# An eight-expert SwiGLU at the end of a two-layer trunk: on-chip memory laid out from a rehearsal, expert weights in rows of 4 and 8 KB, four jobs an expert, a light place first

## The chip, the cores and the metric

One Trainium2 chip, of which the kernel uses one core. A core has five engines that run their own instruction streams side by side: TensorE (PE, matrix products; its weight loads are shown as PEld), VectorE (DVE), ScalarE (ACT), GpSimd (POOL) and SyncE (SP). Here SP issues the loads of weights from HBM into SBUF, the on-chip memory; 16 DMA engines carry them out. Products land in eight PSUM banks. The metric is the device time of one execution in microseconds (us), lower is better.

## The reference, cut to what matters

Two layers of a trunk over 256 context rows and 256 latent rows of width 1024. All of it is in float32.

```
for layer in range(2):                       # layer 1 is the last: latent rows alone from its mixer on
    x = x + g1 * mixer(modulate(rms_norm(x)))
    h = modulate(rms_norm(x))                # 256 x 1024
    layer 0:  x = x + g2 * (silu(h @ w_gate) * (h @ w_up)) @ w_down           # width 2816
    layer 1:  logits = h @ router            # 8 experts, the best two of each row
              gates  = softmax of the two best logits
              for e in range(8):             # w_gate, w_up: 1024 x 3584, w_down: 3584 x 1024
                  out += gates[:, e] * (silu(h @ w_gate[e]) * (h @ w_up[e])) @ w_down[e]
              x = x + g2 * out
return rms_norm(x) * final_norm_g
```

The three matrices of an expert have 44.0 MB, those of the eight experts 352.3 MB. On the inputs that the reference draws, its routing sends 49, 84, 60, 51, 58, 61, 72 and 77 rows to the experts 0 to 7.

## The kernel before

The kernel is written as generators (a mixer, a dense feed-forward, the expert stage `moe`) that a planner, `drive`, interleaves while the program is built. The planner keeps a clock of its own and decides from it the order in which instructions stand on each engine. What waits for what on the chip is settled by semaphores, from the buffers that instructions share.

**Places.** The experts are worked off in eight places, one after the other. A place is heavy (H) or light (L), as `KIND` says, and the places go H L H L H L H L. An H place has room for 128 rows, an L place for 64. The routing (`route`) sorts the experts by how many rows they have; `RANK` tells which place takes which in that order. Expert 0 always comes first in it and has the first place, so that its weights can be loaded before the routing is known (the address of every other place's weights comes from a register that SP loads after the sort, `numbers`). If an expert has more rows than its place has room for, `overflow` computes the rest at the end, behind a branch.

**An H place** multiplies in three products of float32r values: a weight tile `raw` is cut into a high part `wh` (an ACT cast) and a low part `wl` (a DVE subtraction), and the rows likewise (`xeh`, `xel`); `cut_next` and `cut_rest` do this in pieces of 128x1024, of which four are kept (`PIECES`). **An L place** multiplies the float32 weights straight from `raw`, gate and up side by side in the two halves of the array (`pairs`), without cuts.

**Jobs.** A place is seven jobs of 512 of the 3584 hidden columns. A job computes gate and up over eight blocks k of 128 rows (`lin` or `pairs`, into one bank each or one bank in all), then silu on ACT, a product on DVE, and four transposes to the hidden rows' layout (`flip`, bank `pht`), which the second block of the next job's gate carries along (`aside`); `down` multiplies the hidden rows of the job before into the place's banks `y`. Between the blocks `beside` hands in small work: `combine` adds a finished place to the tokens (bank `pcb`), `gather` picks the next place's rows (bank `pxe`).

**Loads.** `moe_units` makes a list of loads of 1 MB, in the order of use: gate and up tiles of 4 blocks by 512 columns (each of the 128 partitions reads four rows of 2 KB), down tiles of 2 blocks by 1024 columns (two rows of 4 KB). `loads` issues the next as soon as there is a buffer. Buffers come from pools: `raws` (4 tiles of 128x2048), one more from `raws2` in layer 1, and, once `early` is set in the second mixer, four tiles of 128x512 from the pool `acts` (63 tiles, which hold activations otherwise) in place of one `raw`; such a load is then issued as four of 128x512, 256 KB each, with rows of 2 KB (`flex`). `SPARE` and `AMAX` bound how many.

```
            if self.free_raw or self.free_raw2:
                self.load(u)
            elif self.early and u["flex"] and self.ACTS - self.live >= 4 + SPARE[self.ap] and self.aheld < AMAX[self.ap]:
                self.aheld += 1
                ...
                u["raw"] = [self.act(name="raw2") for _ in srcs]
```

Every instruction that the planner records on DVE or ACT has line L101, matmuls L244, most transposes L258, loads L202.

## Time and profile before

| | us |
|---|---|
| median of 3 runs | 1777.2 |
| the runs | 1775.42 to 1777.76 |
| the profiled execution's own time | 1777.62 |
| its span, from first to last instruction | 1775.8 |

The profile lists busy time of each engine over the span, and in any stretch of it; what a wait of an engine ended; how much the DMA engines moved; and in order of time what ran. A matmul's end is modelled, so that a short wait inside a run of matmuls can be hidden in busy time. In names such as `gu<-raw,u` the tile written stands left of the arrow. A load's duration on SP is that of its issue.

### The profile page before, as it was taken

What the parts mean: (1) busy time and instruction counts of PE and PEld (TensorE: products, weight loads), DVE (VectorE), ACT (ScalarE), POOL (GpSimd) and SP (SyncE); (2) the same over time, 40 slices, a digit from 0 to 9 for tenths busy, and PEclk for the clock granted to TensorE, in tenths of its full rate; (3) what the DMA queues carried; (4) which work ended last, traced back from release to release, by engine and by line L of the source; (5) the groups of instructions that cost most, each with busy time, mean ns of one, the idle gap of its engine ahead of it and who ended that gap; (6) DMA issues with size and microseconds to landing.
All of it is one profiled execution on the core that took longest, in us unless ns stands there. A gap on an engine that the chain in (4) does not pass through costs nothing. (4 is left out here: it accounts for less than half of the span.)

```text
span 1775.8 us, 25616 instructions
## 1 busy us (share of the span) xinstructions
PE 1713.2 (96%) x8283; PEld 1214.1 (68%) x8283; DVE 1170.0 (66%) x2139; ACT 844.1 (48%) x1620; POOL 2.3 (0%) x9
## 2 busy tenths in 40 slices
PE   7999998999999999999899999999999998999985
PEld 3876776888888888977788536884358842588431
DVE  6899988888764345778699406983069930598412
ACT  3467654444222224566588315872058720477311
POOL 0000000000000000000000000000000000000000
PEclk9899998999999998999999999999999999999999
DMA  9531234456873333226699999999999999999996
GB/s 307 182 129 54 84 125 149 136 170 186 285 242 121 96 89 99 82 95 221 246 357 360 349 392 390 389 379 380 391 389 391 389 387 392 388 373 390 393 387 242
DMA packets 284377, 470.69 MB, mean 265 GB/s; under 512 B 24120, under 2 KB 92236, under 8 KB 284236
## 3 DMA queue, kind: packets, MB, share of 16 engines
q1 hardware_dynamic: 284076, 468.46, 73.8%
q8 instruction: 67, 1.10, 0.3%
q14 instruction: 74, 0.61, 0.1%
q0 software_dynamic: 160, 0.52, 0.1%
HBM read 467.86 MB, written 1.05 MB: 264 GB/s over the span
## 5 line engine op out<-in xcount | busy, mean ns | idle before, releaser
L101 ACT CAST wh<-raw 128x512 fp32r<-128x512 f32 (+4 forms) x708 | 499.9, 743 | 369.7 <-PE pp L244 221.1
L101 DVE TENSOR_TENSOR wl<-raw,wh 128x512 fp32r<-128x512 f32 (+4 forms) x708 | 562.1, 842 | 130.6 <-ACT wh L101 120.3
L244 PE MATMUL gu<-raw,u 128*64 128x512 f32 x896 | 223.3, 604 | 13.2 <-DMA raw<-in_moe_w_up_dram 9.5
L244 PE MATMUL pp<-hh,wh 128*128 128x512 f32 (+1 forms) x592 | 230.2, 389 | 1.5 <-ACT hh L101 1.5
L244 PE MATMUL pp<-hl,wh 128*128 128x512 f32 (+1 forms) x592 | 225.6, 381 | 0.2 <-DVE hl L101 0.2
L244 PE MATMUL pp<-hh,wl 128*128 128x512 f32 (+1 forms) x592 | 225.7, 381 | 0.0
L101 DVE SCALAR_TENSOR_TENSOR macc<-mt,sc,macc 128x512 f32<-128x512 f32 x240 | 169.3, 748 | 27.9 <-DMA mt<-in_w_mod_dram 27.1
L244 PEld LDWEIGHTS gu<-raw,u 128*64 128x64 f32 x896 | 61.7, 137 | 125.3 <-issue 76.8
L101 DVE TENSOR_TENSOR sg<-sg,gu 64x512 f32<-64x512 f32 x28 | 19.4, 692 | 171.4 <-ACT sg L101 171.3
L244 PEld LDWEIGHTS pp<-hh,wh 128*128 128x128 f32 x592 | 112.8, 191 | 23.8 <-ACT hh L101 1.9
L244 PEld LDWEIGHTS pp<-hh,wl 128*128 128x128 f32 x592 | 112.5, 190 | 21.9
L244 PEld LDWEIGHTS pp<-hl,wh 128*128 128x128 f32 x592 | 112.9, 191 | 21.2 <-DVE hl L101 0.7
L244 PE MATMUL y<-raw,hT 128*64 128x512 f32 x448 | 107.3, 596 | 6.4 <-DMA raw<-in_moe_w_down_dram 4.7
L244 PE MATMUL g<-wh,xeh 128*128 128x512 f32 x224 | 92.9, 415 | 1.8 <-ACT wh L101 1.7
L244 PE MATMUL g<-wl,xeh 128*128 128x512 f32 x224 | 87.9, 393 | 3.1 <-DVE wl L101 3.1
L244 PE MATMUL g<-wh,xel 128*128 128x512 f32 x224 | 87.9, 393 | 1.5 <-DVE xel L101 1.5
L244 PE MATMUL u<-wh,xeh 128*128 128x512 f32 x224 | 88.0, 393 | 0.0
L244 PE MATMUL y<-wh,hTh 128*128 128x512 f32 x224 | 87.6, 391 | 0.0
L244 PE MATMUL u<-wl,xeh 128*128 128x512 f32 x224 | 87.3, 390 | 0.0
L244 PE MATMUL y<-wl,hTh 128*128 128x512 f32 x224 | 87.2, 389 | 0.0
L244 PE MATMUL u<-wh,xel 128*128 128x512 f32 x224 | 87.2, 389 | 0.0
L244 PEld LDWEIGHTS y<-raw,hT 128*64 128x64 f32 x448 | 33.1, 137 | 72.7 <-issue 52.9
(327 smaller groups left out, 2541.2 us busy)
## 6 DMA issues: line engine op xcount, KB each, us to landing
raw<-in_moe_w_up_dram SPq DMA_DIRECT2D x300, 256.0 KB, 7.3
raw<-in_moe_w_down_dram SPq DMA_DIRECT2D x292, 256.0 KB, 6.9
raw<-in_moe_w_gate_dram SPq DMA_DIRECT2D x280, 256.0 KB, 6.0
mt<-in_w_mod_dram SPq DMA_DIRECT2D x192, 256.0 KB, 3.3
raw<-in_moe_w_gate_dram SPq DMA_DIRECT2D x42, 1024.0 KB, 8.5
raw<-in_moe_w_down_dram SPq DMA_DIRECT2D x39, 1024.0 KB, 7.3
raw<-in_moe_w_up_dram SPq DMA_DIRECT2D x37, 1024.0 KB, 7.9
raw<-in_ffn_w_down_dram SPq DMA_DIRECT2D x16, 704.0 KB, 4.6
```

The costliest lines, as they stand in the source:

```text
L101: return f(out, *args, **kw)
L244: self.nc.tensor.matmul(out, lhsT, rhs, start=start, stop=stop)
```

## The change

- **SBUF.** The pools `raws`, `raws2`, the pool of cut pieces, `acts` and the pool of modulation weights go. One `Arena` of 104 slots of 128x512 takes their place, in 26 tiles of four slots. The program is built twice: in the rehearsal every request for memory gets a place of its own, and the recording wrappers `Seen` note the first and the last instruction that uses it; `lay_out` then gives each request slots that are free over that stretch, and the second build uses them. A load takes one whole tile of four slots; there is no `flex` any more. To make room, the scratch memory for GpSimd's DMAs is cut to 2 KB, and the final norm's gain comes through eight transposes in place of two GpSimd DMAs.
- **How many loads at a time.** Up to the second mixer four, then five, as before. From the point at which `early` was set (now `wide`) `place_raw` counts slots: loads held, cut pieces, live tiles and a reserve (`SPARE`) have to fit in 104.
- **Jobs.** `WIDE = (2, 2, 2, 1)`: three jobs of 1024 hidden columns and one of 512. A gate or up tile has 2 blocks of 1024 columns (rows of 4 KB; in the last job still 4 blocks of 512, rows of 2 KB). A down tile gives each partition two neighbouring rows of the matrix, 8 KB in one piece, 32 KB away from the next partition's (16 KB in the last job); the hidden columns are transposed in the order that fits. A job fills two banks for gate and two for up in an H place, two in all in an L place.
- **Order.** The places go L H L H H L H L, and `RANK` follows: the experts in the first place, and three with the fewest rows, are light.

```diff
-SPARE, AMAX, ROOM = (10, 3, 3), (13, 12, 9), 62
+SLOT, SLOTS, FOURS, SPARE, ROOM = 512, 104, (5, 3), (16, 26, 26), 62
...
-GATHER_AT = 5
+GATHER_AT = 2
...
-GATES_AT, UDVE = 1, (0, 0, 0, 0)
-KIND, CAP = "HLHLHLHL", dict(H=128, L=64)
-RANK = (0, 4, 1, 5, 2, 6, 3, 7)
+GATES_AT = 0
+KIND, CAP = "LHLHHLHL", dict(H=128, L=64)
+RANK = (0, 1, 5, 2, 3, 6, 4, 7)
+WIDE = (2, 2, 2, 1)
...
+class Arena:
...
+    def take(self, n, dt=F32):
+        i = len(self.uses)
+        self.uses.append([n, self.count, self.count, dt == F32R])
+        if self.rehearsal:
+            s, self.top = self.top, self.top + n
+            t = self.all[:, s * SLOT:(s + n) * SLOT].bitcast(dt)
+        else:
+            s, new = self.layout[i]
+            four = s // 4
+            if new:
+                t = self.tiles[four] = self.pool.tile([128, 4 * SLOT], dt, name=f"four{four}", tag=f"four{four}")
+                self.base[t.tensor.name] = four * 4, 4 * SLOT
+            t = self.tiles[four][:, s % 4 * SLOT:(s % 4 + n) * SLOT]
+        for k in range(n):
+            self.at[s + k] = i
+        return t
...
+def lay_out(uses):
...
+    for i in sorted(range(len(uses)), key=lambda i: (uses[i][1], -uses[i][0])):
+        n, a, b, r = uses[i]
+        best = None
+        for s in range(0, SLOTS, n):
+            last, four = max(end[s:s + n]), s // 4
+            till = max(end[4 * four:4 * four + 4])
+            kind = 4 if four >= SLOTS // 4 - FOURS[0] else 2 if four >= SLOTS // 4 - sum(FOURS) else 1
+            if last >= a or a < wide and (n == 4) != (kind == 4) or till >= a and kinds[four] != r:
+                continue
+            soon = max(0, 50 - (a - last))
...
     def load(self, u):
-        u["pool"] = self.raws if self.free_raw else self.raws2
-        u["raw"] = u["pool"].tile([128, 2048], F32, name="raw", tag="raw")
+        u["raw"] = self.arena.take(4)
+        self.held_raws += 1
+        self.to_cut += len(u["pieces"])
...
+    def place_raw(self, u):
+
+        if not self.wide:
+            return self.held_raws < self.RAWS
+        cut = self.cut - len(self.used)
+        if u["pieces"] or self.cut < self.to_cut:
+            cut = self.PIECES
+        return self.held_raws * 4 + cut * 4 + self.live + 4 <= SLOTS - SPARE[self.ap]
...
-        J = [(e, i) for e in range(NE) for i in range(7)]
+        J = [(e, i) for e in range(NE) for i in range(len(WIDE))]
...
+                u = make((G, U)[w], e, s(0, D), s(f0, f0 + n), "(k p) c -> p k c", s(g, g + kts))
+                h[w] += [(u, k) for k in range(kts)]
...
-            us = [make(Dn, e, i * 512 + g * 256, 0, 2, 1024) for g in range(2)]
-            return [(us[k // 2], k % 2) for k in range(4)]
+            f0, n = sum(WIDE[:i]) * 512, WIDE[i] * 512
+            us = [make(Dn, e, s(f0, f0 + n), s(0, D), "(p k) c -> p k c", s(g, g + 2)) for g in range(0, n // 128, 2)]
+            return [(u, k) for u in us for k in range(2)]
...
-        def pairs(p, gate, up, xs, e, j):
+        def pairs(P, gate, up, xs, e, j):
...
-                self.mm(p[0:64], xs[k], wg(kk), k == 0, k == KT - 1)
-                self.mm(p[64:128], xs[k], wu(kk), k == 0, k == KT - 1)
+                for q, p in enumerate(P):
+                    self.mm(p[0:64], xs[k], wg(kk, q), k == 0, k == KT - 1)
+                    self.mm(p[64:128], xs[k], wu(kk, q), k == 0, k == KT - 1)
...
+            for q in range(WIDE[i]):
+                p = self.ps("pht")
                 for f in range(4):
+                    self.tr(p[:, f * 128:(f + 1) * 128], hid[:, q * 4 + f::n])
```

How instructions move is shown at three places. The first is SP, where the loads of the experts' weights begin, in the second mixer. Before, a row is one load, `raw` the buffer; `128x4x512` is a whole tile, `128x512` a quarter of one:

```order
L202 DMA raw<-in_moe_w_gate_dram 128x4x512 x2
L202 DMA raw<-in_moe_w_up_dram 128x4x512
L202 DMA raw_7575<-in_moe_w_up_dram 128x512
L202 DMA raw_7576<-in_moe_w_up_dram 128x512
L202 DMA raw_7577<-in_moe_w_up_dram 128x512
L202 DMA raw_7578<-in_moe_w_up_dram 128x512
L202 DMA raw_7583<-in_moe_w_gate_dram 128x512
```

The same place of SP now; a tile is called `four` and a number, whatever it holds:

```order
L121 DMA four_6263<-in_moe_w_gate_dram 128x2x1024
L121 DMA four_6626<-in_moe_w_up_dram 128x2x1024
L121 DMA four_6652<-in_moe_w_gate_dram 128x2x1024
L121 DMA four_6666<-in_moe_w_up_dram 128x2x1024
...
L121 DMA four_7040<-in_moe_w_gate_dram 128x2x1024
L121 DMA four_7240<-in_moe_w_up_dram 128x2x1024
L121 DMA four_7242<-in_moe_w_down_dram 128x2048
L121 DMA four_7244<-in_moe_w_down_dram 128x2048
L121 DMA four_7246<-in_moe_w_down_dram 128x2048
L121 DMA four_7248<-in_moe_w_down_dram 128x2048
L121 DMA four_7268<-in_moe_w_gate_dram 128x2x1024
```

The quarters have gone; each load is a tile of 1 MB, gate and up in turn, and twenty of them (sixteen of gate and up, four of down) stand ahead of the first that needs a tile which another load of this stage has held.

The second place is PE at the end of the routing, where the first place's rows are gathered (`pxe`) and its gate begins (`g`). Before:

```order
L244 MATMUL ppos<-mb,oneb 128x8
L244 MATMUL pxe<-OH,tok 128x128 x16
L244 MATMUL g<-wh,xeh 128x512
L244 MATMUL g<-wl,xeh 128x512
L244 MATMUL g<-wh,xel 128x512
```

Now:

```order
L121 MATMUL ppos<-mb,oneb 128x8
L121 MATMUL pxe<-four_7145,four_82 128x64
L121 MATMUL pxe<-four_7145,four_75 128x64
...
L121 MATMUL g<-four_6263,four_7145 64x512
L121 MATMUL g<-four_6626,four_7145 64x512
L121 MATMUL g<-four_6263,four_7145 64x512
L121 MATMUL g<-four_6626,four_7145 64x512
```

There are sixteen gathers of 64 rows in place of sixteen of 128, and the matmuls behind them read the loaded tiles (`four_6263` gate, `four_6626` up) without a cut; each block now takes two products with each.

The third place is PE in an H place, the change from a job's up (`u`) to `down` and the next gate, here in the second place, whose `y` rows still belong to the L place before it; `pht` are the transposes. Now:

```order
L121 MATMUL u<-four_7738,four_7567 128x512 x2
L121 MATMUL y<-four_7586,four_82 64x512 x4
L121 MATMUL y<-four_7588,four_82 64x512 x4
L121 MATMUL g<-four_7546,four_7521 128x512 x2
...
L121 MATMUL g<-four_7757,four_7521 128x512 x2
L121 MATMUL g<-four_7546,four_7521 128x512 x2
L121 MATMUL pht<-idf,four_7618 128x128 x8
```

Products come in twos, one for each bank, and eight transposes stand together where four stood before; an H place has 504 products and 28 transposes either way.

## Rows read from the trace of the kernel before


**Rows 1.** The page: span, busy time of the engines, two groups of loads.

```profile
span 1775.8 us, 25616 instructions
PE 1713.2 (96%) x8283; PEld 1214.1 (68%) x8283; DVE 1170.0 (66%) x2139; ACT 844.1 (48%) x1620; POOL 2.3 (0%) x9
...
raw<-in_moe_w_up_dram SPq DMA_DIRECT2D x300, 256.0 KB, 7.3
raw<-in_moe_w_gate_dram SPq DMA_DIRECT2D x42, 1024.0 KB, 8.5
```

**Rows 2.** The eight places (window and length, PE, PEld, DVE, ACT, POOL, clock, DMA, GB/s).

```profile
873.30:993.80 120.50, 117.75 (x558) 97.11 (x556) 112.99 (x175) 96.75 (x154) 0.00 (x0) 1.00 0.92 332
993.80:1081.10 87.30, 87.30 (x419) 33.85 (x418) 18.14 (x28) 17.29 (x30) 0.00 (x0) 1.00 1.04 386
1081.10:1205.40 124.30, 124.30 (x574) 98.70 (x572) 107.78 (x151) 90.91 (x140) 0.00 (x0) 1.00 1.04 385
1205.40:1298.40 93.00, 89.66 (x420) 34.29 (x419) 20.73 (x35) 15.72 (x30) 0.00 (x0) 1.00 1.04 385
1298.40:1425.80 127.40, 125.30 (x574) 98.52 (x572) 109.30 (x156) 92.83 (x146) 0.00 (x0) 1.00 1.05 391
1425.80:1525.20 99.40, 93.44 (x420) 35.38 (x419) 20.71 (x33) 15.04 (x27) 0.00 (x0) 0.98 1.04 389
1525.20:1653.10 127.90, 125.11 (x572) 98.49 (x570) 109.35 (x156) 93.39 (x146) 0.00 (x0) 1.00 1.04 384
1653.10:1760.40 107.30, 96.98 (x409) 34.43 (x408) 19.93 (x28) 16.16 (x28) 1.23 (x2) 1.00 1.01 374
```

**Rows 3.** Waits of PE, 1653.1 to 1760.4 (total, count, longest).

```profile
PE gu L244 <- DMA raw<-in_moe_w_up_dram: 4.5, 3, 2.6
...
PE gu L244 <- DMA raw<-in_moe_w_gate_dram: 2.7, 3, 1.8
```

**Rows 4.** Waits of PE, 1525.2 to 1653.1.

```profile
PE g L244 <- DVE wl L101: 1.5, 2, 0.8
PE g L244 <- ACT wh L101: 1.1, 1, 1.1
```

**Rows 5.** DVE by form, 1081.1 to 1205.4 (busy, mean ns, idle before).

```profile
L101 DVE TENSOR_TENSOR wl<-raw,wh 128x512 fp32r<-128x512 f32 x98 | 62.1, 688 | 3.1 <-ACT wh L101 2.6
...
L101 DVE TENSOR_TENSOR wl<-raw,wh 128x1024 fp32r<-128x1024 f32 x28 | 33.9, 1224 | 6.1 <-ACT wh L101 5.0
```

**Rows 6.** DMA in 1460 to 1480, 1600 to 1620, 1612 to 1616.5.

```profile
DMA packets 4164, 7.77 MB, mean 389 GB/s; under 512 B 377, under 2 KB 377, under 8 KB 4163
...
DMA packets 3647, 7.93 MB, mean 397 GB/s; under 512 B 290, under 2 KB 290, under 8 KB 3646
...
DMA packets 755, 1.84 MB, mean 410 GB/s; under 512 B 68, under 2 KB 68, under 8 KB 754
```

**Rows 7.** PE in order of time, 993 to 1081.5 (start, duration).

```profile
1001.52 0.50 PE L244 MATMUL y<-wh,hTh 128*128 128x512 f32 x1
...
1007.18 1.94 PE L244 MATMUL gu<-raw,u 128*64 128x512 f32 x8
...
1011.31 0.50 PE L244 MATMUL pcb<-yh,OHT 128*128 128x512 f32 x1
...
1011.97 2.80 PE L244 MATMUL gu<-raw,u 128*64 128x512 f32 x12
...
1028.73 3.60 PE L244 MATMUL y<-raw,hT 128*64 128x512 f32 x16
...
1074.68 2.05 PE L244 MATMUL pxe<-OH,tok 128*128 128x128 f32 x16
```

**Rows 8.** PE in order of time at the end.

```profile
1755.73 0.19 PEld L244 LDWEIGHTS y<-raw,hT 128*64 128x64 f32 x2 [0.49 <-DMA raw<-in_moe_w_down_dram]
...
1758.47 1.94 PE L244 MATMUL y<-raw,hT 128*64 128x512 f32 x8 [1.66 <-SPq L2297]
```

**Rows 9.** The stretch before the stage, columns as in rows 2.

```profile
816.00:873.30 57.30, 52.70 (x413) 46.15 (x412) 39.37 (x105) 28.77 (x66) 0.00 (x0) 0.94 0.86 312
```

More of the change, by code (lines that the diff above doesn't have):

```diff
@@ L102, in __getattr__, with __init__, g @@
         return g
+class Seen:
+    def __init__(self, arena, eng):
+        self.arena, self.eng = arena, eng
+    def __getattr__(self, name):
+        f = getattr(self.eng, name)
+        arena = self.arena
+        def g(*args, **kw):
+            arena.count += 1
+            for x in (*args, *kw.values()):
+                if hasattr(x, "tensor") and arena.has(x):
+                    arena.uses[arena.key(x)][2] = arena.count
+            return None if arena.rehearsal else f(*args, **kw)
+        return g
@@ new lines, in lay_out @@
+def lay_out(uses):
+    end, where, loads, wide, kinds = [-1 << 20] * SLOTS, [None] * len(uses), [], 0, {}
+    for n, a, b, r in uses:
+        if n == 4:
+            loads = [e for e in loads if e >= a] + [b]
+            if len(loads) > FOURS[0]:
+                wide = a
+                break
+    for i in sorted(range(len(uses)), key=lambda i: (uses[i][1], -uses[i][0])):
[8 more added lines that the diff above has]
+            soon = max(0, 50 - (a - last))
+            if n == 4:
+                c = soon, last
+            elif n == 2:
+                c = kind != 2, soon, last
+            else:
+                c = 10 * (a < wide and kind > 1) + soon / 50
+                c += (max(0, b - max(till, a)) if till >= a else b - a + 1000) / (100 if b >= wide or kind > 1 else 2000)
+                c = c, last
+            if best is None or c < best[0]:
+                best = c, s
+        assert best is not None, ("no place", i, uses[i])
+        s = best[1]
+        four = s // 4
+        new = max(end[4 * four:4 * four + 4]) < a
+        where[i], kinds[four] = (s, new), r
+        end[s:s + n] = [b] * n
+    return where
@@ L349, in unit @@
     def unit(self, dmas, size, pieces):
-        u = dict(dmas=dmas, size=size, raw=None, pieces=pieces, left=len(pieces) or 1, flex=None)
+        u = dict(dmas=dmas, size=size, raw=None, pieces=pieces, left=len(pieces) or 1)
         self.units.append(u)
@@ L447, in loads @@
             u = self.units[self.loaded]
-            if u.get("place") and not self.numbers(u["place"]):
+            if u.get("place") and not self.numbers(u["place"]) or not self.place_raw(u):
                 break
-            if self.free_raw or self.free_raw2:
-                self.load(u)
-            elif self.early and u["flex"] and self.ACTS - self.live >= 4 + SPARE[self.ap] and self.aheld < AMAX[self.ap]:
-                self.aheld += 1
-                srcs = u["flex"]() if callable(u["flex"]) else u["flex"]
-                u["raw"] = [self.act(name="raw2") for _ in srcs]
-                for t, src in zip(u["raw"], srcs):
-                    self.dma(t, src, self.t)
-            else:
-                break
+            self.load(u)
             self.loaded += 1
@@ L1350, in projections @@
             if not need:
-                self.early = True
+                self.wide = True
                 self.loads()
@@ L1866, in route @@
         V.tensor_copy(num, self.rank)
-        V.tensor_copy(iod.rearrange("p (j s) -> p s j", s=2), num.rearrange("p (s j) -> p s j", s=2))
+        for e, n in enumerate(RANK):
+            if not e or n != RANK[e - 1] + 1:
+                m = next(k for k in range(1, NE + 1 - e) if e + k == NE or RANK[e + k] != n + k)
+                V.tensor_copy(iod[:, e:e + m], num[:, n:n + m])
         self.ordered = True
@@ L2026, in moe @@
         xe = {0: []}
-        for g in range(2):
+        for g in range(2 if KIND[0] == "H" else 1):
             yield self.hold(1)
@@ L2134, in down @@
                 self.held += n
-            yield self.when(("hT", j))
+            yield self.when(*(wide("hT", j) if not light else [("hT", j, 0)]))
+            n = len(R[j]["d"])
             if light:
```

313 lines of the change are left out of this document (157 added, 156 removed).

## The prediction, made before the result was known

> **What bounds the kernel now.** I read the page first: TensorE is busy 96% of the span, DVE 66%, and there is next to nothing on POOL [rows 1]. That is an average, so I next cut the expert stage into its eight places with the table of windows [rows 2]. It runs from 873.3 to 1760.4, 887.1 us of 1775.8. The reader is to see two kinds of place. In an L place DVE and ACT work some 20 us each and PE needs few weight loads; in an H place DVE works 108 us and ACT 91. The DMA engines are full in every place but the first, at 384 to 391 GB/s. One place holds 42 loads of 1.0486 MB (44.04 MB), so at 387 GB/s it needs 114 us of DMA. An H place takes 124 us of PE, an L place 87: L outruns the loads, H lets them catch up, and a pair is almost exactly balanced. The two places in which PE's busy time equals the length of the window are the second (87.3) and the third (124.3). The other L places took 93.0, 99.4 and 107.3. The waits of PE say why: in the last L place it waited 4.5 and 2.7 us for loads of up and gate [rows 3], and as a matmul's end is modelled, part of a wait is hidden in busy time. In the late H places the stall shows as a late cut, `wl` from DVE and `wh` from ACT [rows 4]: the cut is late because its load is.
>
> So the stage has two limits that lie close together, 387 GB/s of loads and PE. What the change is worth depends on which is left.
>
> **PE's part.** The change keeps the number of products (504 in an H place, 336 in an L place) and 28 transposes a place. If no load is late, four L and four H places take 4 × (87.3 + 124.3) = 846.4 us.
>
> Corrections come from the timeline [rows 7]. The first place has no predecessor: the last `down` of the place before, here 1001.52 to 1007.18, 5.7 us, and four `combine` steps of 0.66 (1011.31 to 1011.97), 2.6 us, fall away: −8.3. The last place has its own last `down` to add, 16 products, 3.6, and some 16 transposes of gains, which I bound by the 16 small products of a gather, 2.05, and take at 1.8; two gathers of 2.05 and about 0.9 of small products for a next place are missing. Together +0.4. The fifth place follows an H place where the row behind 124.3 followed an L place: 5.7 of `down` in place of 3.6, +2.1. Sum 846.4 − 8.3 + 0.4 + 2.1 = 840.6.
>
> Two small things I set against each other. There are three changes of job fewer in a place, 24 in all, which I guess at 3 us together; the entry of an H place, whose first cut pieces must be made before PE can begin, may cost 2. DVE does not become the limit: a cut of 128x1024 takes 1224 ns, two of 128x512 take 1376 [rows 5], so wider cuts spare at most 0.15 us for each pair of the 98 and hide behind PE anyway. If that cover were gone the sum would not move by more than 49 × 0.15 = 7 us a place.
>
> The `down` of a wide job is twice that of a narrow one, 7.2 us in an L place by the 3.6 of sixteen products [rows 7], and 11.4 in an H place by its 5.7. It lies between a job's up and the next gate, so silu, product and transposes of a job have that time to free the banks; I cost the wider hand-over at nothing. The program up to 873.5 keeps the same instructions on PE in the same order; its last stretch has PE busy 52.7 of 57.3 us [rows 9], so loads that start sooner there may cost some us, not tens. I cost it at nothing, and the scratch memory of GpSimd (2.3 us of POOL work in all) too. Eight transposes for the final gain are below half of 2.05.
>
> Behind the last place's products the tail stays: the last `y` begins to end at 1760.4, the span ends at 1775.8, 15.4 us. PE waited 1.7 us of it for SP at the branch [rows 8], which stays.
>
> 873.5 + 840.6 + 15.4 = 1729.5 of span; the profiled run's own time was 1.8 above its span and within 0.5 of the median: **1731**.
>
> **The loads' part.** The loads must deliver 336 × 1.0486 MB. Before the stage begins 57.3 us at 312 GB/s, 17.9 MB, 17 loads, have moved [rows 9]. 319 are left. What is their rate with rows of 4 and 8 KB? The views of DMA give three points [rows 6]. The packets under 512 B are semaphore writes; without them the mean packet is 2.05, 2.36 and 2.68 KB. Mixing rows of 2 and 4 KB gives those means with 0, 26 and 47% of the bytes in rows of 4 KB. Rates: 389, 397, 410 GB/s. A line through them to 90% of the bytes (6/7 of gate and up, all of down, 8 KB counted as 4) gives 417 to 430. Rows of 8 KB are not shown. Bounds: 389, no gain, and 436, the steeper line to its end. I take 410, the fastest that a row shows.
>
> One load then takes 2.557 us; 319 take 815.7, to 1689 if nothing stops them. They are stopped in H places, when all slots are full: 104 less 16 reserve, 16 for cut pieces and some 24 live tiles leave 12 loads. By the pair: an L place draws down 42 − 87.3/2.557 = 8, an H place gives 124.3/2.557 − 42 = 6.6. In the order L H L H H L H L with 17 at the start and 79 us for the first place the stock goes 6, 12 (full), 4, 11, 12 (full), 4, 11, 3: never empty. The two full stretches cost about 16 us of loads, so the last lands at about 1705. From the last landing to the end it took 1755.7 to 1775.8, 20.1 us [rows 8]: 1725, below 1729.5. PE sets the end, by little. This holds down to some 400 GB/s (2.62 us: 873.5 + 836 + 20 = 1730).
>
> The Trainium skill, "SBUF — State Buffer", section "Summary: rules for kernel authors", advises an estimate of about 358 GB/s for transfers between HBM and SBUF. By it 319 loads would take 934 us and the end would be at 1830, slower than the kernel before; the windows of the places show 384 to 391 already with rows of 2 KB, so the measurement decides and I give that no chance.
>
> **Rivals.**
> *The rate does not rise* (0.18). If row length is not what the three points show (the faster stretches may owe it to a tile's larger size), a load takes 2.696 us at 389, 319 take 860, and the end is 873.5 + 860 + 20.1 + 1.8 = **1755**. Still below 1777, since the light place first lets PE draw the stock at once and no place waits for cuts at 332 GB/s, as the first did. Against it: the rate goes up in order with the share.
>
> *The stock is not there* (0.08). If early loads are held back to about 5 until the stage, the first L place waits for 5 + 31 − 42 = −6 loads, 15 us: **1744**.
>
> *Slower: the down loads* (0.06). Each partition now reads 8 KB with 32 KB between neighbours, where before 128 partitions read one contiguous stretch in rows of 4 KB. If such a load takes longer, 207 gate and up loads take 529 us and 112 down loads 112 d. With d a third longer, 3.41 us, the sum is 911 and the end 873.5 + 911 + 20.1 + 1.8 = **1807**. It decides at 1781, where d is 3.18 us, 330 GB/s. No row shows such a pitch. The Trainium skill, "DMA: Bandwidth & Descriptors", section "Latency and other measured facts", reports that rows a large power of two apart are read slower: 207 GB/s at 512 KiB and 164 at 2 MiB, where a padded pitch had 214. No row here and no figure there is near 32 KB; by 164 against 214 d would be 3.34 and the end about 1798.
>
> *Slower: banks* (0.02). An H place holds two banks each of gate, up and `y`, and one or two for `pht` and `pcb`: none spare. The next gate waits if silu and product (two of each for one before) outlast the 11.4 us of `down`. To reach 1781 each of the 16 jobs of the H places would have to wait 3.1 us (50 us in all); ACT and DVE have 30 and 15 us free in a place.
>
> *Nothing happens* (0.03): gains and small losses in H entries cancel: **1776**.
>
> *Better* (0.05): the rate is above 420 and fewer job changes are worth over 2 us a place: **1710**.
>
> **How the numbers follow.** The main case has 0.58, with a range of its own of 1720 to 1744: below by the 3 us of job changes and a mean of 1 us a place, above by a rate just under 400 or H entries of 3 us. For the range I reach to the flat rate and its bounds, 1712 to 1760; outside lie slower, nothing and better, 0.16. Some 3.6 us, 0.2%, is about what a measurement here can tell from no change. Faster: 0.58 + 0.18 + 0.08 + 0.05 = 0.89; same 0.03; slower 0.08.
>
> **What would show it.** Right: L places of 87 to 89 us each and H places of 124 to 126, no wait of PE for loads above 1 us, DMA at 400 or more in L places and below 400 in H places that are full, the stage beginning within 2 us of 873.5. Wrong: DMA still at 389 with its share of time at 1 and PE waiting for `raw` in L places (flat rate); down loads of gate-like size that take over 3 us each (pitch); PE waiting for ACT's silu or DVE's product at each job (banks); a late start of the stage (early loads in the mixer's way).

## The result, and the profile after

The changed kernel takes **1749.2 us** (median of 4 runs, 1745.53 to 1750.29), the kernel before 1777.5 beside it: a ratio of 0.9837, 95% interval 0.9818 to 0.9856. The forecast was 1731, with a range of 1712 to 1760. The direction and the mechanism were right, the gain of 28 us was three fifths of the 46 expected.

The page of the profiled execution (1749.87 us), to be held against [rows 1]:

```profile
span 1748.1 us, 22827 instructions
PE 1707.2 (98%) x8291; PEld 1224.1 (70%) x8291; DVE 1153.9 (66%) x1928; ACT 811.9 (46%) x1388; POOL 1.1 (0%) x7
...
four<-in_moe_w_gate_dram SPq DMA_DIRECT2D x112, 1024.0 KB, 12.9
four<-in_moe_w_up_dram SPq DMA_DIRECT2D x112, 1024.0 KB, 13.8
four<-in_moe_w_down_dram SPq DMA_DIRECT2D x112, 1024.0 KB, 13.8
```

The eight places, L H L H H L H L, in the table of windows, columns as in [rows 2]:

```profile
878.40:960.70 82.30, 82.27 (x393) 30.88 (x393) 17.39 (x38) 13.32 (x20) 0.00 (x0) 0.96 0.93 368
960.70:1085.20 124.50, 124.50 (x574) 99.26 (x572) 99.28 (x97) 85.27 (x95) 0.00 (x0) 1.00 0.97 371
1085.20:1172.90 87.70, 87.70 (x420) 35.21 (x419) 20.69 (x30) 14.05 (x21) 0.00 (x0) 1.00 1.03 410
1172.90:1301.35 128.45, 125.81 (x573) 99.05 (x571) 110.89 (x111) 91.60 (x101) 0.00 (x0) 1.00 0.99 396
1301.35:1427.00 125.65, 124.19 (x581) 103.25 (x579) 109.73 (x109) 89.35 (x97) 0.00 (x0) 1.00 0.95 363
1427.00:1515.30 88.30, 87.95 (x419) 35.13 (x418) 20.79 (x30) 14.17 (x21) 0.00 (x0) 1.00 1.03 411
1515.30:1643.80 128.50, 125.86 (x572) 98.88 (x570) 105.41 (x104) 87.10 (x95) 0.00 (x0) 1.00 1.02 404
1643.80:1733.60 89.80, 89.45 (x417) 33.95 (x416) 19.88 (x26) 16.74 (x25) 0.00 (x0) 1.00 0.95 379
```

In [rows 2] the later L places grew from 87.3 to 107.3 us while DMA stood at 374 to 391 GB/s. Now the later L places take 87.7, 88.3 and 89.8, at 410 where the queue stays full, and some places have DMA engines idle (0.95). The waits of PE over the whole stage (total, count, longest) name no load any more, where [rows 3] had two:

```profile
PE g L121 <- DVE four L121: 6.4, 6, 1.5
PE g L121 <- ACT four L121: 1.4, 2, 0.7
PE y L121 <- DVE four L121: 0.7, 2, 0.3
PE u L121 <- DVE four L121: 0.5, 2, 0.3
```

And the rate itself, in three stretches of 8 us with a full queue: 1144 to 1152 (rows of 2 KB), 1164 to 1172 (4 KB), 1210 to 1218 (8 KB), as in [rows 6]:

```profile
DMA packets 1553, 3.10 MB, mean 387 GB/s; under 512 B 46, under 2 KB 46, under 8 KB 1551
...
DMA packets 851, 3.28 MB, mean 410 GB/s; under 512 B 51, under 2 KB 51, under 8 KB 851
...
DMA packets 467, 3.34 MB, mean 418 GB/s; under 512 B 54, under 2 KB 54, under 8 KB 64
```

So the loads stopped being the bound. The missing gain is in PE's time: the stage from the first `g` to the last `y` takes 855 us, where 840.6 were forecast, and it begins at 878.4, not 873.5 (in the profile of before, 873.3).

### The profile page after: what moved, and what is told of

Read it like the earlier page. It is cut to its first block, busy times and chain, and to the rows that moved or that the text cites. A ratio compares the mean times of both kernels' runs of the same rounds, so it can differ in the third digit from the quotient of the medians.

```text
span 1748.1 us, 22827 instructions
## 1 busy us (share of the span) xinstructions
PE 1707.2 (98%) x8291; PEld 1224.1 (70%) x8291; DVE 1153.9 (66%) x1928; ACT 811.9 (46%) x1388; POOL 1.1 (0%) x7
## 5 line engine op out<-in xcount | busy, mean ns | idle before, releaser
L121 DVE TENSOR_TENSOR four<-four,four 128x1024 fp32r<-128x1024 f32 (+9 forms) x633 | 622.5, 1017 | 239.9 <-ACT four L121 199.0
L121 ACT CAST four<-four 128x1024 fp32r<-128x1024 f32 (+7 forms) x564 | 507.1, 934 | 432.3 <-PE pp L121 197.0
L121 PE MATMUL pp<-four,four 128*128 128x512 f32 (+1 forms) x2678 | 592.7, 381 | 4.4 <-ACT four L121 3.4
L121 PEld LDWEIGHTS pp<-four,four 128*128 128x128 f32 x2678 | 479.8, 191 | 100.5 <-ACT four L121 4.6
L121 PE MATMUL g<-four,four 128*64 128x512 f32 (+1 forms) x1532 | 370.0, 519 | 7.7 <-DVE four L121 6.4
L121 PEld LDWEIGHTS g<-four,four 128*64 128x64 f32 (+1 forms) x1532 | 176.5, 159 | 153.0 <-issue 112.5
L121 PE MATMUL y<-four,four 128*128 128x512 f32 (+1 forms) x1088 | 252.5, 474 | 0.7 <-DVE four L121 0.7
L121 PEld LDWEIGHTS y<-four,four 128*128 128x128 f32 (+1 forms) x1088 | 151.4, 167 | 90.6 <-issue 61.6
L121 PE MATMUL u<-four,four 128*128 128x512 f32 x630 | 151.6, 392 | 0.5 <-DVE four L121 0.5
L121 DVE SCALAR_TENSOR_TENSOR four<-four,sc,four 128x512 f32<-128x512 f32 x213 | 150.9, 747 | 0.9
L121 ACT ACTIVATE four<-psc,nm 128x512 f32<-128x512 f32 (+1 forms) x72 | 43.7, 614 | 20.5 <-DVE nm L121 15.2
```

The costliest lines, as they stand in the source:

```text
L121: return None if arena.rehearsal else f(*args, **kw)
```

## The experiments

Twelve kernels were run. What the program before the stage takes differs from profile to profile: its last transposes, behind the same PE instructions in the same order, start anywhere from 856.1 to 861.7 (861.3 in the one above, 859.5 in that of before). The granted clock of PE goes with it. The changed kernel, in two stretches (columns as in [rows 2], the clock third from the end):

```profile
40.00:50.00 10.00, 10.00 (x51) 7.72 (x49) 7.89 (x22) 3.13 (x6) 0.00 (x0) 0.73 1.02 306
...
690.00:700.00 10.00, 10.00 (x33) 8.12 (x34) 9.97 (x28) 4.78 (x11) 0.00 (x0) 0.67 0.00 0
```

and e1, the first experiment below, whose transposes start at 856.5:

```profile
40.00:50.00 10.00, 10.00 (x61) 7.64 (x60) 9.54 (x28) 3.13 (x6) 0.00 (x0) 0.97 1.04 311
...
690.00:700.00 10.00, 10.00 (x44) 8.22 (x43) 7.19 (x21) 4.11 (x9) 0.00 (x0) 0.95 0.01 2
```

Held against e1 product by product, the changed kernel falls back by 3.0 us between 41 and 66 us, by 1.6 between 674 and 699 and by 0.6 between 776 and 797, and keeps step within 0.4 us elsewhere up to the transposes. The four profiles of changed kernels that start latest (the one above, e8, e12, e13) are those with the lowest clock from 25 to 65 us, 0.79. Executions of one kernel differ in the same way: e1 took 1741.4 and 1741.9 us at a mean granted clock of 0.984, and 1746.0 and 1747.0 at 0.981. Why the clock falls more in one execution than in another is not shown.

So the medians below also hold this difference of some 5 us, and the intervals of most ratios overlap that of the changed kernel. The argument rests on the lengths of the places, which agree within 0.2 us between runs wherever an edit does not reach. Lengths are taken from the first `g` of a place to that of the next, the last one to the start of its last `y` (0.4 us before its end, to which [rows 2] counts); "stage" is their sum, "tail" what follows. Theories A and B are those of the text that stands ahead of each result. The entry of an H place is the time of its first products, until PE no longer waits for cut pieces.

| run | median us | start | places in order, us | stage | tail |
|---|---|---|---|---|---|
| before | 1777.5 | 873.3 | H120.4 L87.3 H124.3 L93.0 H127.4 L99.4 H128.0 L106.9 | 886.7 | 15.7 |
| changed | 1749.2 | 878.4 | L82.3 H124.5 L87.7 H128.5 H125.6 L88.4 H128.5 L89.7 | 855.1 | 14.5 |
| e1_order | 1744.0 | 870.3 | H120.4 L87.7 H125.9 L88.4 H126.8 L88.4 H128.5 L89.7 | 855.9 | 14.0 |
| e2_jobs | 1749.4 | 873.2 | L83.2 H124.6 L88.8 H125.7 H124.2 L89.0 H125.8 L94.8 | 856.2 | 17.4 |
| e3_down | 1742.8 | 874.8 | L80.5 H124.1 L86.5 H128.1 H125.5 L87.2 H128.3 L90.2 | 850.4 | 17.4 |
| e4_soon | 1745.7 | 873.6 | L82.3 H124.4 L87.7 H128.7 H125.6 L88.4 H128.8 L89.8 | 855.7 | 13.9 |
| e5_pulse | 1743.9 | 873.3 | L79.4 H124.5 L87.7 H128.4 H125.6 L88.4 H128.5 L89.8 | 852.3 | 14.5 |
| e7_shallow | 1750.2 | 873.7 | L81.6 H124.4 L87.8 H128.5 H125.6 L88.4 H128.9 L92.7 | 857.9 | 17.1 |
| e8_stock | 1749.3 | 878.2 | L82.3 H127.7 L88.4 H128.0 H125.6 L88.4 H127.7 L89.8 | 857.8 | 13.9 |
| e10_rate | 1742.3 | 874.8 | L81.8 H124.5 L87.7 H126.8 H123.9 L93.6 H124.4 L89.1 | 851.8 | 13.9 |
| e11_best | 1741.9 | 873.9 | L78.2 H124.1 L88.1 H126.5 H123.8 L95.0 H124.1 L87.6 | 847.5 | 15.2 |
| e12_hfirst | 1752.7 | 879.5 | H117.4 L90.3 H124.1 L86.5 H124.5 L90.8 H125.0 L97.1 | 855.6 | 17.0 |
| e13_two | 1741.1 | 877.7 | L78.2 H124.1 L86.5 H128.0 H125.5 L87.2 H128.2 L89.5 | 847.2 | 17.5 |

**e1, the old order of places.**

```diff
-SLOT, SLOTS, FOURS, SPARE, ROOM = 512, 104, (5, 3), (16, 26, 26), 62
+SLOT, SLOTS, FOURS, SPARE, ROOM = 512, 104, (5, 3), (24, 26, 26), 62
...
-KIND, CAP = "LHLHHLHL", dict(H=128, L=64)
-RANK = (0, 1, 5, 2, 3, 6, 4, 7)
+KIND, CAP = "HLHLHLHL", dict(H=128, L=64)
+RANK = (0, 4, 1, 5, 2, 6, 3, 7)
```

> The changed kernel with the places in the old order, H L H L H L H L; rows, tiles, jobs and layout stay (the reserve ahead of the stage is 24 slots for 16, two loads fewer, for the cut pieces that a heavy first place needs). Theory A, the loads got faster (403 to 416 GB/s where the queue is full) and PE now sets the end in nearly every place: the order matters little, 1745 to 1757 us, with DMA above 400 GB/s in L places and waits of PE for loads under 3 us a place. Theory B, the light place first, which draws a stock that stood unused, gave the gain: 1765 us or more, with PE waiting for loads in the late L places again.

1743.96 us, ratio 0.982 (0.9796 to 0.9845). The stage is as long as with the new order, and no wait of PE names a load; theory B fell. With faster loads the light place first is not what gained the time. It even has a price, which the opening shows. PE in order of time, at the end of the routing, in the changed kernel:

```profile
868.92 0.20 PE L121 MATMUL ppos<-mb,tri 128*128 128x8 bf16 x2 [2.22 <-DVE mb L121]
...
869.83 4.10 PE L121 MATMUL pxe<-four,four 128*128 128x64 f32 x18 [0.63 <-DVE four L121]
...
878.43 8.28 PE L121 MATMUL g<-four,four 128*64 128x512 f32 x24 [1.51 <-DVE four L121]
```

and with the heavy place first (e1):

```profile
865.08 3.90 PE L121 MATMUL pxe<-four,four 128*128 128x128 f32 x18 [0.63 <-DVE four L121]
...
870.29 1.17 PE L121 MATMUL g<-four,four 128*128 128x512 f32 x4
```

From the first gather to the first `g` it is 8.6 us against 5.2. That is 3.4 of the 8.1 us by which e1's stage begins earlier; the rest lies ahead of the routing, as above. PE's granted clock says why, in windows of 5 us. The changed kernel:

```profile
865.00:870.00 5.00, 2.15 (x22) 1.98 (x22) 3.72 (x26) 1.99 (x4) 0.00 (x0) 0.73 0.99 412
870.00:875.00 5.00, 5.00 (x24) 5.00 (x25) 1.97 (x17) 0.00 (x0) 0.00 (x0) 0.50 0.01 4
875.00:880.00 5.00, 3.49 (x14) 2.26 (x15) 2.53 (x9) 0.00 (x0) 0.00 (x0) 0.50 0.00 0
880.00:885.00 5.00, 5.00 (x16) 1.47 (x14) 0.00 (x0) 0.00 (x0) 0.00 (x0) 0.57 0.00 2
```

e1:

```profile
865.00:870.00 5.00, 4.92 (x29) 4.92 (x30) 3.45 (x21) 1.64 (x5) 0.00 (x0) 0.65 0.00 2
870.00:875.00 5.00, 3.94 (x20) 3.00 (x20) 4.47 (x10) 4.02 (x8) 0.00 (x0) 1.00 0.00 0
```

In both the clock falls to half, 1.2 of 2.4 GHz, while PE waits in the routing. In e1, with 128-row gathers, it is back within the gather, after some 7 us; in the changed kernel, with 64-row gathers, the whole gather and the first products of the place run at half clock, which lasts about 17 us. The other kernels of the table with a light first place and no edit to the routing (e2, e3, e4, e7, e8, e10) all have the same 8.6 us from gather to `g`.

**e5, PE kept busy in the routing.**

```diff
+    def pulse(self, n):
+        p = self.ps("warm")
...
+        for _ in range(n):
+            self.nc.tensor.matmul(p.rearrange("p (a b) -> p a b", a=4), self.idb, self.idb.unsqueeze(1).to_broadcast([128, 4, 128]), start=True, stop=True)
+            self.t += 216.0
...
+PULSE = 14, 4, 8
...
+        self.pulse(PULSE[0])
...
+        self.pulse(PULSE[1])
...
+            self.pulse(PULSE[2])
```

> The changed kernel with PE given something to do while it waits in the routing: 14 products of bf16 128x512 into a bank that nobody reads behind plg, 4 behind ppos, 8 behind the first gather. Theory A, the opening is slow since PE's clock falls to 1.2 GHz in the routing and the light first place's 64-row gather brings it back late (some 17 us at 0.5 against 7 with a heavy first place): with the clock held, gather and first place lose 6 us, so 1739 to 1745 us, and the granted clock is 0.9 or more from 865 to 885. Theory B, the pulses are no remedy (the clock stays at 0.5 there): 1748 to 1753.

1743.85 us, ratio 0.9809 (0.9779 to 0.9839). The same windows, now with the clock at 0.95 and 1:

```profile
865.00:870.00 5.00, 5.00 (x37) 3.31 (x35) 2.60 (x20) 0.34 (x1) 0.00 (x0) 0.95 0.14 58
870.00:875.00 5.00, 5.00 (x31) 2.79 (x32) 2.65 (x10) 0.00 (x0) 0.00 (x0) 1.00 0.02 5
...
880.00:885.00 5.00, 5.00 (x26) 1.72 (x24) 0.00 (x0) 0.00 (x0) 0.00 (x0) 1.00 1.02 412
```

The first 24 products of `g` take 5.37 us, not 8.28, and the first place 79.4, not 82.3; the forecast had 79.0 for it. Of the 4.9 us that the stage began late, the gather at half clock is 3.4; the rest lies ahead of the last transposes. Theory A holds for the clock and for the 6 us that gather and first place lose. The pulses take some of it back, which I had not counted: from the last transposes to the first gather it is now 10.9 us, where the changed kernel has 8.5. So 3.7 us are left, 2.9 of them in the stage, and the early start in this profile (873.3) is mostly the clock before the routing.

**e2, seven jobs.**

```diff
-GATHER_AT = 2
+GATHER_AT = 4
...
-WIDE = (2, 2, 2, 1)
+WIDE = (1, 1, 1, 1, 1, 1, 1)
```

> The changed kernel with seven jobs of 512 hidden columns an expert, as before: rows of gate and up are 2 KB again, those of down stay 8 KB, 16 KB apart; loads of 1 MB, layout and the new order of places stay. Theory A, longer rows make the loads faster: 389 to 397 GB/s in stretches of gate and up, some 400 over a place, just enough for PE: 1752 to 1762 us. Theory B, whole tiles of 1 MB instead of quarters of 256 KB make them faster and not the row: 405 GB/s or more in gate and up too, and 1745 to 1752 us.

1749.35 us, ratio 0.9848 (0.9828 to 0.9869): no different from the changed kernel. The rate went back as theory A has it, 397 GB/s over a place (here the third and the sixth):

```profile
1081.10:1169.90 88.80, 88.80 (x420) 35.36 (x419) 18.73 (x29) 13.49 (x23) 0.00 (x0) 1.00 1.04 398
...
1419.80:1508.80 89.00, 89.00 (x420) 35.30 (x419) 21.22 (x31) 16.36 (x26) 0.00 (x0) 1.00 1.04 397
```

so whole tiles are not what made gate and up faster: rows of 2 KB in whole tiles read at 387 GB/s in the stretch shown above too. But its time was better than I gave it. 319 loads at 397 GB/s take 843 us, still less than PE's 855: only the last place ran into loads (94.8, with one wait of 1.7 us for `up`). The step from 387 to 397 fits down rows at 418 for a third of the bytes, and it pays, as far as e6 below shows what 387 would cost; the step from 397 to 410, from the wider jobs, buys slack. What the wider jobs save in L places (88.8 to 87.7 in the third) they lose at the H entries, which are 2.8 us shorter here.

**e3, down rows of 4 KB again.** The hidden columns are transposed in runs instead of every eighth (or fourth) one.

```diff
-            us = [make(Dn, e, s(f0, f0 + n), s(0, D), "(p k) c -> p k c", s(g, g + 2)) for g in range(0, n // 128, 2)]
+            us = [make(Dn, e, s(f0, f0 + n), s(0, D), "(k p) c -> p k c", s(g, g + 2)) for g in range(0, n // 128, 2)]
...
-                    nc.tensor.transpose(p[:, f * 64:(f + 1) * 64], hid[r, f::n], self.idf[r, r])
+                    nc.tensor.transpose(p[:, f * 64:(f + 1) * 64], hid[r, f * 128:(f + 1) * 128], self.idf[r, r])
...
-                    self.tr(p[:, f * 128:(f + 1) * 128], hid[:, q * 4 + f::n])
+                    self.tr(p[:, f * 128:(f + 1) * 128], hid[:, (q * 4 + f) * 128:(q * 4 + f + 1) * 128])
```

> The changed kernel with the down tiles read as before, two rows of 4 KB to a partition from one contiguous stretch each; the rest stays. Theory A, PE sets the end: 1746 to 1753 us, the rate in full stretches 400 to 412 GB/s in place of 403 to 416. The rival, that rows 32 KB apart are read slower, gives a shorter time here, 1744 or less, with down loads landing sooner.

1742.77 us, ratio 0.9808 (0.9788 to 0.9827). That is the time which I had put down as the rival's sign, rows 32 KB apart being slow, but its cause is another. Of the 6.4 us below the changed kernel 4.7 are in the stage. The loads did not get faster (406 GB/s in its third and sixth place, where the changed kernel had 410 and 411; 418 for the 8 KB rows above). Each L place is 1.2 to 1.8 us shorter until the last, and the transposes of the hidden rows show it (PE in groups by shape over the stage: busy, mean ns). The changed kernel:

```profile
L121 PE MATMUL pht<-idf,four 64*128 64x64 f32 x112 | 15.9, 279 | 0.0
```

e3:

```profile
L121 PE MATMUL pht<-idf,four 64*128 64x64 f32 x112 | 10.3, 230 | 0.0
```

Eight of them take 1.09 us when they read every eighth column, and 0.70 when they read a run: 14 such groups, 5.5 us. The change's 8 KB rows cost this on PE. The last place does not gain (90.2), as its last products of `y` wait three times, 1.3 us in all, for loads it seems (see e7). The 128-row transposes of H places differ by only half a microsecond in all. The Trainium skill, "DMA: Bandwidth & Descriptors", section "Latency and other measured facts", has rows slowed at pitches that are large powers of two, from 512 KiB up. At 32 KB, with rows of 8 KB, the trace has the highest rate of all three row lengths; e3 alters row length and pitch together, so the pitch alone was not tried.

**e4, the layout's cost of a new tile.**

```diff
-            soon = max(0, 50 - (a - last))
+            soon = max(0, 50 - (a - (till if till < a else last)))
```

> The changed kernel with one term of the layout's cost altered: where a request starts a new tile of four slots, the distance is counted from the last use of any of the four and not of its own slots alone, since a new tile waits for all of them. Theory A, the entries of the fourth and seventh place lose some 4 us each since a cut piece waits for a neighbour's slot: 1738 to 1745 us, H entries after L of 124.5 in place of 128.5. Theory B, those entries wait for loads, of which only two are ahead there: 1747 to 1753, no change.

1745.68 us, ratio 0.9826 (0.9805 to 0.9847), but the entries of the fourth and seventh place are unchanged (128.7 and 128.8); the profile's gain is a start 4.8 us earlier, with the transposes ahead of the routing at 856.5, which is the clock named above. Theory A fell, since this term of the layout's cost was not the cause; whether loads are late there, as theory B has it, the next runs ask.

**e7, four loads fewer in the stock, by the count of slots.**

```diff
-SLOT, SLOTS, FOURS, SPARE, ROOM = 512, 104, (5, 3), (16, 26, 26), 62
+SLOT, SLOTS, FOURS, SPARE, ROOM = 512, 104, (5, 3), (16, 42, 42), 62
```

> The changed kernel with a reserve of 42 slots for 26 from the stage on, so that four loads fewer are held ahead (some 8 for 12 in H places). Theory A, an L place draws down 8 loads and the stalls at the entry of the fourth and seventh place are late loads: with four fewer they grow by up to 10 us for each of the L places that start from a full H stock, 1760 to 1785 us, waits of PE for loads in L places. Theory B, those stalls are cut work that is late for another reason, and the stock is ample: 1748 to 1754.

1750.21 us, ratio 0.9839 (0.9811 to 0.9868). Entries again 128.5 and 128.9, with two loads fewer issued ahead (11 and 13, for 13 and 15, at the start of the third and the sixth place). Only the last place grew, by 3 us: its last four groups of eight products of `y`, the products of one down load each, start 2.4 to 2.6 us apart, as far as a load takes, with 2.0 us of waits that the profile puts down to SP. So theory B holds: up to there the stock is ample, and the entry stall did not grow with fewer loads. What it is, ACT shows in order of time in the changed kernel, where the fourth place begins at 1172.9:

```profile
1167.37 1.04 ACT L121 CAST four<-four 128x1024 fp32r<-128x1024 f32 x1 [0.61 <-DMA four<-in_moe_w_gate_dram]
1174.13 3.89 ACT L121 CAST four<-four 128x1024 fp32r<-128x1024 f32 x4 [5.71 <-PE g L121]
```

The first two pieces belong to one load, which is there at 1167.4; yet the second cut waits for products of `g` of the place itself. It stands behind them in the program; since buffers alone settle what waits for what, it must take a buffer that they read (a reading, not tried by itself). One piece is cut when PE comes, not four.

**e8, a larger reserve ahead of the stage,** meant to leave eight loads fewer there.

```diff
-SLOT, SLOTS, FOURS, SPARE, ROOM = 512, 104, (5, 3), (16, 26, 26), 62
+SLOT, SLOTS, FOURS, SPARE, ROOM = 512, 104, (5, 3), (48, 26, 26), 62
```

> The changed kernel with a reserve of 48 slots for 16 ahead of the stage, so that some 8 loads fewer are there when it begins. Theory A, the light first place needs the stock (9 + 31 - 42 is -2): PE waits some 5 us for loads in the first place and the entry of the second is late, 1753 to 1763 us. Theory B, the stock is not needed since loads at 410 GB/s and more catch up: 1747 to 1752.

1749.33 us, ratio 0.9831 (0.9798 to 0.9863). The edit did not do what it was meant to. From 800 to 878 us the same 18 loads are issued in both kernels, and the DMA view of that stretch has the same row in both:

```profile
DMA packets 4390, 18.96 MB, mean 243 GB/s; under 512 B 288, under 2 KB 288, under 8 KB 3872
```

The loads came later (106 GB/s from 800 to 820 us where the changed kernel has 292, then 353 where it has 170), but 21 have been issued in both when the stage begins. So the time says nothing about the stock, and whether the first place needs it stays untested; neither theory was put to the test. What the run does show is that the entry of the second place grew by 3.2 us, with waits for DVE and ACT and none for DMA. ACT in order of time there, the place beginning at 960.5:

```profile
954.34 1.04 ACT L121 CAST four<-four 128x1024 fp32r<-128x1024 f32 x1
961.73 1.99 ACT L121 CAST four<-four 128x1024 fp32r<-128x1024 f32 x2 [6.34 <-PE g L121]
```

It is the order of the fourth place again, one piece cut ahead and the next behind products of `g`, where the changed kernel cuts two ahead. The planner takes the loads to be later than they are; that this wrote the late cuts is argued here and tried in e10.

**e10, the planner's rate.** `dma` reckons with 365 GB/s; the chip gives 410.

```diff
-        self.dt = max(self.dt, free) + k * 4 / 365.0
+        self.dt = max(self.dt, free) + k * 4 / (410.0 if self.wide else 365.0)
```

> The changed kernel with one number of the planner's clock altered: loads are reckoned at 410 in place of 365 GB/s once the tiles are counted by slots. It puts the cuts of an H place's first pieces ahead of its first products; before, the second cut stood behind the products of the first block. Theory A, the fourth and the seventh place lose 4 us each by that written order, neither by late loads (four fewer in stock left them at 128.5) nor by the layout's cost: H entries after L at 124.5 to 126, total 1739 to 1745 us. Theory B, the loads are late there after all, so cuts ahead wait on the queue and PE with them: 1746 to 1753, or slower.

1742.27 us, ratio 0.9808 (0.9791 to 0.9826). The fourth, sixth and seventh place:

```profile
1168.80:1295.60 126.80, 124.70 (x572) 99.31 (x572) 113.61 (x116) 91.20 (x100) 0.00 (x0) 1.00 1.01 402
...
1419.40:1513.00 93.60, 89.51 (x419) 35.45 (x418) 20.48 (x30) 13.12 (x20) 0.00 (x0) 0.98 1.03 410
1513.00:1637.50 124.50, 124.50 (x574) 99.22 (x572) 105.49 (x104) 89.12 (x96) 0.00 (x0) 1.00 1.02 403
```

The seventh place lost its stall entirely (128.5 to 124.5), the fourth 1.7 us of it and the fifth 1.7: the written order was the cause, in the fourth place at least in part. But the sixth place gave 5 us back. ACT in order of time there, and the wait of PE that it became:

```profile
1500.34 1.99 ACT L121 CAST four<-four 128x1024 fp32r<-128x1024 f32 x2 [18.54 <-DMA four<-in_moe_w_gate_dram]
1502.85 1.04 ACT L121 CAST four<-four 128x1024 fp32r<-128x1024 f32 x1 [0.52 <-DMA four<-in_moe_w_gate_dram]
1503.80 0.58 ACT L121 COPY four<-pht 128x512 f32<-128x512 f32 x1
```

```profile
PE y L121 <- ACT four L121: 4.1, 1, 4.1
```

A cut that stands ahead of its load blocks ACT, and the copy of the hidden rows behind it, for which `y` waits. The truth lies between the theories: the order costs some 7 us in three H places, and at 410 the planner is too hopeful in one L place, where it costs 5. The stage gains 3.3.

**e11, e12, e13, edits together.** e11 is e3, e5 and e10 in one; e12 the same with the old order of places and e1's reserve; e13 e3 and e5 alone.

> The changed kernel with three edits together: the planner's 410 GB/s, down rows of 4 KB (which spare the transposes their stride, 6 us measured) and the products that keep PE's clock up in the routing (4 us of the stage). If the causes are separate and PE sets the end in every place, the gains add: stage 838 to 843 us, total 1727 to 1736. If a place runs into the loads' rate (409 GB/s for rows of 4 KB, where 420 was read for 8), the sum falls short: 1737 to 1743, with PE waiting for loads in the late L places.

> The same three edits with the old order of places H L H L H L H L (reserve ahead of the stage 24 slots). If the order matters nothing once PE sets the end, 1727 to 1738 us, as the light place first; if the light place first is what lets PE use the stock of loads at the faster pace, the old order is now slower by 5 us or more and its late L places wait for loads.

> The changed kernel with two of the edits, down rows of 4 KB and the products that hold PE's clock in the routing; the planner reckons with 365 GB/s again, so that no cut stands ahead of its load and ACT is not held up by one in an L place (with 410 a wait of 4 to 7 us stood in the sixth place). If the two gains add, stage 846 to 848 us and total 1735 to 1741, the same as with all three or a little less; if the planner's number was worth its 3 us in the sum of three, this one is at 1743 to 1746.

e11 1741.9 us (ratio 0.98, 0.9782 to 0.9819), e13 1741.12 (0.9805, 0.9791 to 0.9818), both below the changed kernel's 1749.2, by intervals that just meet its own, and level with e3 alone (1742.8) and e10 alone (1742.3). The stages do add: 855.1 less 4.7 (e3) less 2.8 (e5) is 847.6, and 847.2 was measured. The time does not follow in full. Against the changed kernel, the tail of e13 takes 3.0 of those 7.9 us back (17.5 for 14.5); against e3, its profile has the transposes ahead of the routing 4.0 us later (861.4 for 857.4). In that tail `pcb` waits 3.0 us for DVE, in the changed kernel 0.9; e2, e3, e7 and e12 have it too (3.0 to 3.4). In all five, and in no other kernel with the change, the last products of `y` wait as in e7 (0.3 to 3.4 us in all): there the last place meets the loads again. What DVE waits for is PE's sequencer at the branch for `overflow`, as in the changed kernel; why that comes later was not tried, and e11 has a wait of 2.2 us without late products. In e11 the blocked ACT costs more than in e10 (the sixth place 95.0), which takes back what the H places gain.

e12, 1752.74 (0.9857, 0.9835 to 0.9879), is slower by 11 us than the light place first with the same edits, of which 8 are in the stage. Its last L place takes 97.1 us, with waits for loads (`up` 1.6, `gate` 0.9). The rest is not the order: its transposes start 4.1 us later than e11's, and the pulses, given twice by the two gathers of a heavy place, put off its start. So the order of places is worth some 8 us after all, but only once PE is fast enough to meet the loads again. e1 alone would have said that it is worth nothing.

**e6, the order alone in the kernel before.**

```diff
-KIND, CAP = "HLHLHLHL", dict(H=128, L=64)
-RANK = (0, 4, 1, 5, 2, 6, 3, 7)
+KIND, CAP = "LHLHHLHL", dict(H=128, L=64)
+RANK = (0, 1, 5, 2, 3, 6, 4, 7)
```

> The kernel before with the new order of places alone (L H L H H L H L and its ranks); pools, quarter tiles, seven jobs and 2 KB rows stay. Theory A, loads at 387 GB/s bind it, and a light first place uses their stock at once, where a heavy one let the queue stand full: 1752 to 1764 us, the rival of the prediction with a flat rate. Theory B, the order is worth nothing without faster loads, as it was worth nothing with them (the old order measured no slower): 1772 to 1780.

3270.61 us, which is no measure of the order: the old code maps experts to places for H and L in turn alone, so the expert with 84 rows landed in a light place, the kernel computed another assignment, and the branch for overflow ran for 1500 us behind the stage. The eight places themselves run the same instructions whatever the routing, and can be read: L80.6 H124.3 L97.1 H126.7 H124.2 L92.0 H126.4 L105.4, the last `y` at 1755.5, 876.7 us of stage against 886.7, at 385 to 390 GB/s in every later place. PE's waits in the third place:

```profile
PE gu L244 <- DMA raw<-in_moe_w_up_dram: 2.5, 3, 1.5
PE y L244 <- DMA raw<-in_moe_w_down_dram: 1.6, 2, 1.0
```

At 387 GB/s the loads bind in either order, and the order alone is worth some 10 us of the stage, not the 22 that the rival with a flat rate had (1777 to 1755). This stays a reading of one profile, with another assignment of experts.

## Why the prediction was right in kind and short in size

- **The bound and its removal: right.** Loads held up PE in the old L places; with longer rows they do not. I took 410 GB/s; the trace has 387, 410 and 418 for rows of 2, 4 and 8 KB, so the line through [rows 6] was good, and the guess that 8 KB reads as 4 KB was on the low side. "PE sets the end, by little" was right also in its second half: e2 shows that 397 is just enough, e12 that it can tip back. No run has the old row lengths in gate, up and down at once with the rest of the change, so that the rows and nothing else lifted the bound is argued from these rates.
- **The flat rate, the missing stock and the down pitch** as rivals: all fell. The stock was there, with 21 loads issued when the stage began, where the rival had about 5 loads. Whether it was needed is open, since e8 did not take it away.
- **Two readings behind this were wrong, without harm to the forecast.** "A pair is almost exactly balanced" does not follow from its own numbers: two places need 2 × 114 = 228 us of loads at 387 GB/s and 87 + 124 = 211 of PE; at 410 they need 215, and there it holds. And the stock in H places was reckoned with the reserve of 16 slots, which `SPARE` has only up to the stage's first job; with the 26 that follow the same sum gives 9 loads, not 12, and still never reaches zero.
- **The sum of PE's part failed: 840.6 for 855.1.** It was made of 4 × (87.3 + 124.3), and these two rows, the best of each kind before, were held for what every place would take. Four things were mis-sized.
 - The first place, 79.0: measured 82.3, since I priced its products at full clock. The gather ahead of it lost another 3.4: I had "the program up to 873.5 keeps the same instructions", but its last step, the gather, goes from 128 rows to 64. Held up, the clock gave 79.4 (e5).
 - H entries, "may cost 2", set against 3 us of job changes: measured 4.2 in each of two places. The order in which the planner writes cuts comes from a rate that it believes in, not the one the chip has (e10, which took away all of it in one place and part of it in the other).
 - "28 transposes a place" were kept in number and not in price: with every eighth column they cost 5.5 us over the L places (e3), which hid what fewer job changes gain. Without them L places are 86.5 and 87.2, for 87.3; the guess of 3 us in all fits that, but was not measured by itself.
 - The last place: 89.7 for 87.7, of which the transposes are a part (87.6 in e11, 89.1 in e10); the rest was not taken apart.
- **Banks, wider cuts, GpSimd's memory**: no row shows a cost, as priced. The H place without a stall takes 124.1 to 124.5, the row of before.
- **The tail**: 14.2 for 15.4, from the end of the last `y`. The 1.7 us of [rows 8] that I counted in it stood ahead of the last products, within the last place, and the changed kernel has no such wait.
- **The start**: 878.4 for 873.5, of which 3.4 the gather and the rest the clock ahead of the routing, which differs between executions. That the stage began near 873.5 in other runs is this clock's doing, not the forecast's.

## What to carry to other kernels

When a bound is lifted, price the next one by what each stretch does in the new arrangement and not by the best stretch of the old: operand strides, a clock that falls in a pause, and an order written from a planner's belief about the loads had no row in the old profile and took most of the 18 us that are missing from the 46. A faster resource wants its number corrected in the planner as well, and with care, since an instruction put ahead of its data blocks what stands behind it on its engine. And an edit that measures as nothing (the order in e1) may be worth 8 us when another limit moves (e12). Last, look whether an edit did what it was for before reading its time: in e8 the stock that was to shrink did not.

## What the runs showed of the hardware

- The read rate rises with the length of the contiguous run for each partition, at the same 1 MB a load: 387, 410 and 418 GB/s for 2, 4 and 8 KB in stretches with a full queue. The runs of 8 KB start 32 KB apart and are no slower for it than e3's down rows of 4 KB from one contiguous stretch (406 GB/s over a place, where the changed kernel has 410).
- 64-row float32 transposes that read every eighth column take 1.09 us for eight, against 0.70 from a run of columns; for 112 transposes of 128 rows it is 15.5 against 15.0 us.
- PE's clock fell to half in the routing. Where gathers of 128 rows came next (e1) it stayed there for some 7 us, where gathers of 64 rows did, for some 17.
- The same PE instructions ahead of the stage take 856 to 862 us, and the difference falls where the granted clock differs (0.73 against 0.97 at 40 to 50 us, 0.67 against 0.95 at 690 to 700).
